# A transformer-like layer on one core: batch 1's T4 sums last and on GpSimd, other PSUM banks, an earlier slab split, moved down-stage casts

## The chip, the cores and the metric

The kernel runs on one core of one Trainium2 chip. The metric is the device time of one execution in microseconds. The engines are TensorE (PE in the profile; its weight loads are PEld), VectorE (DVE), ScalarE (ACT), GpSimd (POOL) and SyncE (SP), which issues nearly all DMAs. Each engine works through its own list of instructions in order, and waits on semaphores for the others.

## The reference

Two batches of 512 tokens, each of width 1024, go through one layer with shared weights; all is float32.

```python
xn = rmsnorm(x, norm1_g);  proj = xn @ w_in          # lru_x, lru_gate, q, k, v, gates
xc = dwconv(lru_x);  h = rglru_fwd(xc) + rglru_bwd(xc)
a_out = (gelu(lru_gate) * h) @ w_lru_out              # 1280 -> 1024
o = three dilated window attentions, combined by a softmax over their lse
b_out = o @ w_att_out                                 # 512 -> 1024
x = x + (sig(g_a) * a_out + sig(g_b) * b_out) @ w_o
xn2 = rmsnorm(x, norm2_g)
gate, val = split(xn2 @ w_up)                         # 1024 -> 3072 each
x = x + (gelu(dwconv(gate)) * val) @ w_down           # 3072 -> 1024
```

## The kernel before

Every product is made of three matmuls on pairs (hi, lo): each float32 operand is cast by ACT to a hi tile, and a subtraction on DVE or GpSimd makes the lo tile; then hi by hi, hi by lo and lo by hi are added up in PSUM (L1048 to L1050, L1196 to L1198, L1315 to L1317). Weights come as slabs of 128 by 512 through one stream, `ws`: `ws.adv(n)` splits up to n slabs ahead (load on SP, cast on ACT at L227, lo at L230 on the engine that `lo_eng` names in turn), at most eight slabs of a ring being alive and at most three loads ahead of the splits. `ws.take` hands them out and `ws.done` gives their place back.

The stages follow each other. The projections and the recurrence come first, then attention, then the gelu of the LRU gate with the combine of the three attention groups (`combine`, L872 to L879, the store of its result `o_d` at L879). These last steps are deferred functions, run by `tick()`; the loop `while later: tick()` drains them.

Then the mixing stage: `mix_tile(b, c)` makes, for each batch b and eight column tiles c, `a_out` and `b_out` in one two-bank PSUM tile (tag `m`, two buffers) and scales them with the gates `tha` and `thb` loaded by `th_load` (L980; DVE L1000 to L1004). `gain2`, the norm's gain for 128 partitions, is loaded at L1023. `o_phase` multiplies by `w_o` (`o_group`), and adds the result to the accumulator `acc[t]` of a tile of 128 tokens (DVE L1053). `load_acc` fills those accumulators with x.

The feed-forward part uses a scheme of seven products of half width for one 128-column tile f of gate and value (f from 0 to 23), in place of eight: for batch 0 the operands B11 and B21, for batch 1 sums of both batches called T1, T2, T3, T4 and B22. `batch0(f)` makes the products with B11 and B21, `rest(f, pa)` those with T2, T1, T3, B22 and T4, in this order, on PSUM banks of tag A, B and C. ACT copies between them: `u` (L1230) reads bank A after T2, and T3 writes that bank again; `p` (L1235) reads bank C after T1, and B22 writes it again. The weights of the products are sums too (L259, DVE), from four loads of `w_up` for each f (L245). From f = 0 to 3 (`EARLY`) batch 0's products come ahead of the others. After each product `prod` calls `ws.adv(2)`. The gelu (`gc`, L1243 to L1255) ends in the store of f's row to DRAM, `f_d` (L1256).

The operands of batch 1 are made tile by tile (four tiles of 128 tokens) in `sums_T`: eight transposes of the normalised tile into a two-bank PSUM tile `pst` (L1123), then sums by DVE and GpSimd (L1128) and casts by ACT (L1131 to L1148). It is a generator: each `sums(i)` runs tile i's next piece. `own_sums(i)` takes the squares for the norm (ACT L1014, whose output `junk` takes a PSUM tile of tag `m`), `own_scale(i)` applies it (DVE L1020). The table `after` and the lines ahead of the loop over f set which pieces stand between which products:

```python
6: lambda: (ws.adv(4), own_scale(2), sums(1, ps3, "m"), sums(0)),
7: lambda: (own_sums(3), sums(1), own_scale(3), lo_eng.remove(V), ws.adv(4)),
...
banks[0] = batch0(0, mid=lambda: (sums(2, ps4, "t"), sums(1)))
sums(2)
banks[1] = batch0(1)
sums(2)
sums(3, ps4, "t")
batch0(2, "C")
sums(3)
ws.hold = len(specs)
lo_eng[:] = [G]
batch0(3, "C", lambda: sums(3))
```

At the end, `h_fetch` loads rows of `f_d` again, `h_pair(f, engs)` casts two of them and makes their lo tiles (ACT L1272, L1273 on DVE for the first and GpSimd for the second), and the down stage multiplies them by `w_down` on eight PSUM banks (`psd`) and adds to the accumulators (DVE L1318).

Of the kernel before, what the change touches and what calls it, by code (L numbers as in the profile page):

```python
# [113 lines left out]
def layer_kernel(ctx: ExitStack, tc: tile.TileContext, xs_in, norm1_g, w_in, conv_w, conv_b, lru_wa, lru_ba,  # L114
# [791 lines left out]
    for c in range(KR):  # L906
# [43 lines left out]
        step[0] += 1  # L950
    while later:
        tick()
# [70 lines left out]
    SP.dma_start(out=gain2, in_=norm2_g[0].partition_broadcast(128))  # L1023
# [41 lines left out]
    lo_eng[:] = [V, G]  # L1065
    ws.adv(8)
    for c in range(KD):
        mix_tile(0, c)
        if c == 3:
            load_acc(0)  # L1070
    x2["B11"], x2["B21"] = half_pair(x20p, "B11"), half_pair(x20p, "B21")
# [46 lines left out]
    def sums_T(i, pst):  # L1118
# [7 lines left out]
        b12, b22, t1, t3 = v(pst[:, 0]), v(pst[:, 1]), v(x_t[:, 0:512]), v(x_t[:, 512:1024])  # L1126
        t2 = st.tile([128, 4, 128], F32, tag="t2", bufs=1, name="t2")
# [3 lines left out]
        A.copy(out=t3, in_=b12)  # L1131
        A.copy(out=hi("B22"), in_=b22)
        sub(V, t1, b12, hi("B11"))
        sub(V, t1, t1, lo("B11"))
        sub(V, t2, b22, t1)
        A.copy(out=hi("T1"), in_=t1)
        A.copy(out=hi("T2"), in_=t2)
        yield
        sub(V, t3, b22, t3)
        sub(V, lo("T1"), t1, hi("T1"))  # L1140
        sub(V, lo("T2"), t2, hi("T2"))
        sub(V, lo("B22"), b22, hi("B22"))
        A.copy(out=hi("T3"), in_=t3)
        sub(G, t1, hi("B21"), t2)
        sub(G, t1, t1, lo("B21"), ALU.add)
        sub(G, lo("T3"), t3, hi("T3"))
# [7 lines left out]
    def sums(i, pool=None, tag=None):  # L1154
# [13 lines left out]
        6: lambda: (ws.adv(4), own_scale(2), sums(1, ps3, "m"), sums(0)),  # L1168
# [13 lines left out]
    cm_ps, ps4 = open_pool("ps4", space=PSUM)  # L1182
    cm_ps_ab, ps4ab = open_pool("ps4ab", space=PSUM)
# [3 lines left out]
    g0s, p1 = {}, {}  # L1187

    def prod(ps, slab, op, start, free=True):
# [9 lines left out]
        if free:  # L1199
            ws.done("a", 1)  # L1200
            ws.adv(2)

    bank = lambda nm: (ps4 if nm == "C" else ps4ab).tile([128, 512], F32, tag=nm, bufs=2, name="pf" + nm)
# [15 lines left out]
    def rest(f, pa):  # L1219
# [16 lines left out]
        prod(pa, ws.take(1)[0], "T3", False)  # L1236
        V.tensor_tensor(out=p5, in0=p5, in1=pa, op=ALU.add)
# [40 lines left out]
    banks[0] = batch0(0, mid=lambda: (sums(2, ps4, "t"), sums(1)))  # L1278
    sums(2)
    banks[1] = batch0(1)  # L1280
    sums(2)
    sums(3, ps4, "t")
    batch0(2, "C")
    sums(3)
    ws.hold = len(specs)
    lo_eng[:] = [G]
    batch0(3, "C", lambda: sums(3))
    close(cm_st)
    for f in range(NF):
        if f == NF - 1:  # L1290
            for j in range(4):
                h_fetch(j)
        pa = banks.get(f) if f < EARLY else batch0(f)
        if f == NF - 1:
            h_pair(0, (V, G))
# [68 lines left out]
```

## Time and profile before

| | |
|---|---|
| time, median of three runs (lowest to highest) | 2123.88 us (2123.47 to 2126.91) |
| the profiled execution: time, and span in the trace | 2123.89 us, 2122.1 us |
| TensorE busy | 2032.0 us, 96% of the span |
| VectorE, ScalarE, GpSimd busy | 61%, 41%, 33% |
| HBM traffic over the span | 100 GB/s |
| chain that ended last, by engine | PE 75%, DVE 12%, issue 4%, ACT 4%, POOL 2%, DMA 2% |

All times in the rows are microseconds from the start of the span. An engine's busy share says how much of the span it worked; where TensorE is idle, the row that follows the gap names in brackets how long it sat idle and what released it.

### The profile page before, as it was taken

How to read it: one execution, taken by the hardware profiler on the slowest of the kernel's cores; microseconds unless marked ns; L12 is line 12 of the kernel's file. 1: busy time of each engine (PE TensorE's matmuls, PEld its weight loads, DVE VectorE, ACT ScalarE, POOL GpSimd, SP SyncE). 2: the span in 40 equal slices, each digit the busy share in tenths (PEclk: the TensorE clock that was granted, in tenths of full speed). 3: DMA queues.
4: the chain of work that ended last, by engine and by line, in shares of the span. 5: the costliest groups of instructions: out<-in, count | busy, mean ns of one | idle time of the engine just before them, and what ended most of it. 6: DMA issues, size and time to landing. Idle time of an engine off the chain costs nothing.

```text
span 2122.1 us, 26424 instructions
## 1 busy us (share of the span) xinstructions
PE 2032.0 (96%) x9571; PEld 1710.5 (81%) x9571; DVE 1296.6 (61%) x1874; ACT 873.1 (41%) x1501; POOL 691.7 (33%) x583
## 2 busy tenths in 40 slices
PE   8988898999999999999998999979999999999999
PEld 6866676787899999998776888757888888788887
DVE  5599998617862671575565565656555555465555
ACT  4488888622331243135442342433444444421210
POOL 3111111034113421423332122464545554532421
PEclk9999999999999999999999999989999999999999
DMA  4535444411111111103546556323222222352322
GB/s 146 156 99 143 115 127 131 158 45 43 34 41 46 40 51 55 35 16 120 163 159 209 170 165 196 106 76 92 89 75 85 90 80 90 121 196 80 109 90 80
DMA packets 204032, 218.71 MB, mean 103 GB/s; under 512 B 28892, under 2 KB 148222, under 8 KB 203902
## 3 DMA queue, kind: packets, MB, share of 16 engines
q1 hardware_dynamic: 201854, 211.78, 32.2%
q0 software_dynamic: 2048, 5.25, 1.0%
q8 instruction: 75, 1.23, 0.2%
q14 instruction: 55, 0.45, 0.1%
HBM read 161.73 MB, written 50.00 MB: 100 GB/s over the span
## 4 chain that ended last, share of the span: by engine, by line
PE 75%; DVE 12%; issue 4%; ACT 4%; POOL 2%; DMA 2%; SPq 0%; DVEq 0%; POOLq 0%; ACTq 0%
PE ps L807 7%; PE ps L808 6%; PE ps L809 6%; PE ps L151 5%; PE ps L152 5%; PE ps L153 5%; PE psd L1315 4%; PE psd L1317 4%; PE psd L1316 4%; PE pfA L1196 4%; PE pfA L1197 3%; PE pfA L1198 3%; DVE u L486 3%; PE o L728 3%; PE pfC L1196 2%
## 5 line engine op out<-in xcount | busy, mean ns | idle before, releaser
L230 POOL TENSOR_TENSOR lo<-raw,hi 128x512 fp32r<-128x512 f32 (+1 forms) x261 | 344.6, 1331 | 668.1 <-ACT hi L227 635.4
L227 ACT CAST hi<-raw 128x512 fp32r<-128x512 f32 (+1 forms) x352 | 204.8, 606 | 310.0 <-PE psd L1317 152.5
L807 PE MATMUL ps<-hi,xh 128*128 128x512 f32 x576 | 251.4, 437 | 0.0
L808 PE MATMUL ps<-lo,xh 128*128 128x512 f32 x576 | 228.5, 397 | 0.0
L809 PE MATMUL ps<-hi,xl 128*128 128x512 f32 x576 | 228.3, 396 | 0.0
L151 PE MATMUL ps<-xh,hi 128*128 128x512 f32 x544 | 217.8, 400 | 0.3 <-DVE xc L403 0.3
L152 PE MATMUL ps<-xl,hi 128*128 128x512 f32 x544 | 216.1, 397 | 0.0
L153 PE MATMUL ps<-xh,lo 128*128 128x512 f32 x544 | 215.4, 396 | 0.0
L1318 DVE TENSOR_TENSOR accd<-accd,psd 128x512 f32<-128x512 f32 x192 | 130.1, 686 | 110.8 <-PE psd L1317 104.4
L807 PEld LDWEIGHTS ps<-hi,xh 128*128 128x128 f32 x576 | 156.2, 271 | 9.6
L808 PEld LDWEIGHTS ps<-lo,xh 128*128 128x128 f32 x576 | 158.4, 275 | 6.0
L809 PEld LDWEIGHTS ps<-hi,xl 128*128 128x128 f32 x576 | 156.4, 271 | 8.0
L1315 PE MATMUL psd<-hi,hp 128*128 128x512 f32 x384 | 149.7, 390 | 0.4 <-DVE gc L1255 0.4
L1316 PE MATMUL psd<-lo,hp 128*128 128x512 f32 x384 | 149.4, 389 | 0.0
L1317 PE MATMUL psd<-hi,hp 128*128 128x512 f32 x384 | 149.4, 389 | 0.0
L707 ACT ACTIVATE p<-p,nm 128x128 f32<-128x128 f32 (+1 forms) x192 | 81.7, 427 | 146.4 <-DVE nm L705 146.3
L629 DVE TENSOR_REDUCE ss<-sq 128x8 f32<-128x512 f32 x48 | 32.9, 685 | 163.7 <-ACT sq L626 163.7
L1196 PE MATMUL pfA<-T,hi 128*128 128x512 f32 x288 | 116.0, 403 | 15.4 <-ACT u L1230 9.0
L151 PEld LDWEIGHTS ps<-xh,hi 128*128 128x128 f32 x544 | 104.9, 193 | 24.5 <-issue 1.2
L153 PEld LDWEIGHTS ps<-xh,lo 128*128 128x128 f32 x544 | 104.7, 192 | 22.7
L152 PEld LDWEIGHTS ps<-xl,hi 128*128 128x128 f32 x544 | 104.9, 193 | 22.1
L1198 PE MATMUL pfA<-T,lo 128*128 128x512 f32 x288 | 115.3, 400 | 0.9 <-POOL lo L230 0.9
(255 smaller groups left out, 4532.2 us busy)
## 6 DMA issues: line engine op xcount, KB each, us to landing
raw<-in_w_in_dram SPq DMA_DIRECT2D x144, 256.0 KB
raw<-in_w_up_dram SPq DMA_DIRECT2D x56, 256.0 KB
r<-in_w_up_dram SPq DMA_DIRECT2D x48, 256.0 KB
f_d<-gc SPq DMA_DIRECT2D x24, 512.0 KB
raw<-in_w_down_dram SPq DMA_DIRECT2D x48, 256.0 KB
hraw<-f_d SPq DMA_DIRECT2D x24, 512.0 KB
sg_d<-sgt SPq DMA_DIRECT2D x16, 512.0 KB
raw<-in_w_lru_out_dram SPq DMA_DIRECT2D x32, 256.0 KB
```

Of the source, the lines that this page charges most:

```text
L151: PE.matmul(out=ps, lhsT=a, rhs=b, start=(k == 0), stop=False)
L152: PE.matmul(out=ps, lhsT=a, rhs=rl(k), start=False, stop=False)
L153: PE.matmul(out=ps, lhsT=wl(k), rhs=b, start=False, stop=(k == n - 1))
L227: A.copy(out=hi[:, 0:n], in_=r[:, 0:n])
L230: e.tensor_tensor(out=lo[:, 0:n], in0=r[:, 0:n], in1=hi[:, 0:n], op=ALU.subtract)
L807: PE.matmul(out=ps, lhsT=a, rhs=hi, start=(k == 0), stop=False)
L808: PE.matmul(out=ps, lhsT=a, rhs=lo, start=False, stop=False)
L809: PE.matmul(out=ps, lhsT=b, rhs=hi, start=False, stop=(k == KD - 1))
L1196: PE.matmul(out=ps, lhsT=a, rhs=bh[:, k], start=(start and k == 0), stop=False, **kw)
L1315: PE.matmul(out=ps, lhsT=hh[:, i, tl], rhs=w[0], start=(i == 0), stop=False)
L1316: PE.matmul(out=ps, lhsT=hh[:, i, tl], rhs=w[1], start=False, stop=False)
L1317: PE.matmul(out=ps, lhsT=hl[:, i, tl], rhs=w[0], start=False, stop=(i == 1))
```

## The change

The change has four parts.

1. **Mixing start.** `lo_eng` is set to DVE and GpSimd in turn before the deferred functions are drained, and `ws.adv(8)` is called there too, besides the call at the old place. `gain2` is loaded not at L1023 but behind `load_acc(0)`, in the fourth tile of batch 0. In what is issued, one cast, one DVE lo and one LRU half-slab load (128 KB, ahead of the two `o_d` stores and one `y_d` store on SP) come earlier.
2. **Sums of batch 1.** The pieces of `sums_T` are cut anew. First DVE makes t1 and t2, ACT copies bank 0 to t3 and casts T1 and T2, and DVE makes T2's and T1's lo; second come B22 and T3, with both lo tiles on DVE; third two GpSimd sums for T4; last T4's cast and its lo on GpSimd. Before, the two T4 sums and T3's lo were one piece. t3 has a tile of its own and t2 takes half of the token tile. The calls of the pieces stand in other places, with the T4 pieces of tiles 1 to 3 ahead of `rest(0)`.
3. **Banks and pace.** In place of two PSUM pools there are four, opened in the order C, B, t, A. `prod` advances the stream by `pace[0]`: 1 in `batch0(0)` to `batch0(2)`, 2 in `batch0(3)`, 1 in `rest(0)` to `rest(3)`, and 2 from f = 4.
4. **Down-stage casts.** `h_pair(0, (V, G))` is called inside `rest(23)`, behind the T3 product, and no longer ahead of `rest(23)`.

The core of the diff:

```diff
+    lo_eng[:] = [V, G]
+    ws.adv(8)
     while later:
...
-    SP.dma_start(out=gain2, in_=norm2_g[0].partition_broadcast(128))
     def norm2_tile(t):
...
-    lo_eng[:] = [V, G]
             load_acc(0)
+            SP.dma_start(out=gain2, in_=norm2_g[0].partition_broadcast(128))
...
             PE.transpose(out=pst[:, k // 4, 128 * (k % 4):128 * (k % 4) + 128], in_=x_t[:, 128 * k:128 * k + 128],
                          identity=ident)
         v = lambda ap: ap.rearrange("p (k t) -> p k t", t=128)
-        b12, b22, t1, t3 = v(pst[:, 0]), v(pst[:, 1]), v(x_t[:, 0:512]), v(x_t[:, 512:1024])
-        t2 = st.tile([128, 4, 128], F32, tag="t2", bufs=1, name="t2")
+        b12, b22, t1, t2 = v(pst[:, 0]), v(pst[:, 1]), v(x_t[:, 0:512]), v(x_t[:, 512:1024])
+        t3 = st.tile([128, 4, 128], F32, tag="t3", bufs=1, name="t3")
         sub = lambda eng, out, x, y, op=ALU.subtract: eng.tensor_tensor(out=out, in0=x, in1=y, op=op)
         hi = lambda nm: x2[nm][0][:, :, tl]
         lo = lambda nm: x2[nm][1][:, :, tl]
-        A.copy(out=t3, in_=b12)
-        A.copy(out=hi("B22"), in_=b22)
         sub(V, t1, b12, hi("B11"))
         sub(V, t1, t1, lo("B11"))
         sub(V, t2, b22, t1)
+        A.copy(out=t3, in_=b12)
         A.copy(out=hi("T1"), in_=t1)
         A.copy(out=hi("T2"), in_=t2)
+        sub(V, lo("T2"), t2, hi("T2"))
+        sub(V, lo("T1"), t1, hi("T1"))
         yield
+        A.copy(out=hi("B22"), in_=b22)
         sub(V, t3, b22, t3)
-        sub(V, lo("T1"), t1, hi("T1"))
-        sub(V, lo("T2"), t2, hi("T2"))
+        A.copy(out=hi("T3"), in_=t3)
         sub(V, lo("B22"), b22, hi("B22"))
-        A.copy(out=hi("T3"), in_=t3)
+        sub(V, lo("T3"), t3, hi("T3"))
+        yield
         sub(G, t1, hi("B21"), t2)
         sub(G, t1, t1, lo("B21"), ALU.add)
-        sub(G, lo("T3"), t3, hi("T3"))
         yield
         A.copy(out=hi("T4"), in_=t1)
         sub(G, lo("T4"), t1, hi("T4"))
...
-        6: lambda: (ws.adv(4), own_scale(2), sums(1, ps3, "m"), sums(0)),
+        6: lambda: (ws.adv(4), own_scale(2), sums(1, ps3, "m")),
         7: lambda: (own_sums(3), sums(1), own_scale(3), lo_eng.remove(V), ws.adv(4)),
...
-    cm_ps, ps4 = open_pool("ps4", space=PSUM)
-    cm_ps_ab, ps4ab = open_pool("ps4ab", space=PSUM)
+    cm_pf, pf = zip(*(open_pool("ps4" + nm, space=PSUM) for nm in "CBtA"))
+    pf = dict(zip("CBtA", pf))
+    pace = [1]
     def prod(ps, slab, op, start, free=True):
...
-            ws.adv(2)
-
-    bank = lambda nm: (ps4 if nm == "C" else ps4ab).tile([128, 512], F32, tag=nm, bufs=2, name="pf" + nm)
+            ws.adv(pace[0])
+
+    bank = lambda nm: pf[nm].tile([128, 512], F32, tag=nm, bufs=2, name="pf" + nm)
     def batch0(f, nm="A", mid=None):
...
-    def rest(f, pa):
+    def rest(f, pa, mid=None):
...
         prod(pa, ws.take(1)[0], "T3", False)
+        if mid:
+            mid()
...
 
     ws.loads()
     banks = {}
-    banks[0] = batch0(0, mid=lambda: (sums(2, ps4, "t"), sums(1)))
+    banks[0] = batch0(0, mid=lambda: sums(2, pf["t"], "t"))
     sums(2)
     banks[1] = batch0(1)
+    sums(3, pf["t"], "t")
+    sums(0)
+    sums(0)
+    batch0(2, "C")
+    ws.hold = len(specs)
+    pace[0] = 2
+    lo_eng[:] = [G]
+    sums(1)
+    batch0(3, "C", lambda: sums(3))
+    sums(1)
     sums(2)
-    sums(3, ps4, "t")
-    batch0(2, "C")
+    sums(2)
     sums(3)
-    ws.hold = len(specs)
-    lo_eng[:] = [G]
-    batch0(3, "C", lambda: sums(3))
+    sums(3)
     close(cm_st)
+    pace[0] = 1
     for f in range(NF):
         if f == NF - 1:
             for j in range(4):
                 h_fetch(j)
+        if f == EARLY:
+            pace[0] = 2
         pa = banks.get(f) if f < EARLY else batch0(f)
-        if f == NF - 1:
-            h_pair(0, (V, G))
-        rest(f, pa)
-    close(cm_f, cm_b, cm_ps_ab, cm_ps)
+        rest(f, pa, (lambda: h_pair(0, (V, G))) if f == NF - 1 else None)
+    close(cm_f, cm_b, *cm_pf[::-1])
 
 
     cm_ps, ps5 = open_pool("ps5", space=PSUM)
```

How the instructions move, at three places.

ACT ahead of `rest(0)`, before. T4's casts are the rows with T4; `u2` is the copy of bank A between T2 and T3; `hi` rows are weight casts, those from `s1`, `s2` and `r21` of weight sums:

```order
L1211 COPY p1_11640<-pfC_11612 128x512
L1148 CAST T4_11028<-acc_10704 128x4x128
L227 CAST hi_11656<-r21_11464 128x512
L227 CAST hi_11668<-raw_11462 128x512
L227 CAST hi_11691<-r22_11466 128x512
L227 CAST hi_11699<-s2_11696 128x512
L1230 COPY u2_11676<-pfA_11468 128x512
L227 CAST hi_11718<-s1_11695 128x512
```

And after:

```order
L227 CAST hi_11664<-raw_11462 128x512
L1150 CAST T4_11028<-acc_10700 128x4x128
L1150 CAST T4_11028<-acc_10702 128x4x128
L1150 CAST T4_11028<-acc_10704 128x4x128
L227 CAST hi_11697<-r22_11466 128x512
L1233 COPY u2_11682<-pfA_11468 128x512
L227 CAST hi_11718<-s2_11715 128x512
```

Before, one T4 cast (tile 3's) stands there, five rows ahead of `u2`. After, three T4 casts (tiles 1 to 3) stand in a row, with one weight cast between them and `u2`. On GpSimd, T4's sums and lo of tiles 1 to 3 with four weight lo's among them are the operations behind tile 0's T4 lo.

SP around the store of f = 3's row, before. `f_d` rows are the stores of the rows 2, 3; the `w_up` rows between are loads for f = 5, those behind for f = 6:

```order
L245 DMA r22_11950<-in_w_up_dram 128x4x128
L1256 DMA f_d_68<-gc_12008 128x1024
L245 DMA raw_12076<-in_w_up_dram 128x4x128
L245 DMA raw_12095<-in_w_up_dram 128x4x128
L245 DMA r21_12097<-in_w_up_dram 128x4x128
L245 DMA r22_12099<-in_w_up_dram 128x4x128
L1256 DMA f_d_68<-gc_12119 128x1024
L245 DMA raw_12228<-in_w_up_dram 128x4x128
```

And after, with the loads of f = 5 behind both stores:

```order
L245 DMA r22_12016<-in_w_up_dram 128x4x128
L1261 DMA f_d_68<-gc_11988 128x1024
L1261 DMA f_d_68<-gc_12101 128x1024
L245 DMA raw_12147<-in_w_up_dram 128x4x128
L245 DMA raw_12153<-in_w_up_dram 128x4x128
L245 DMA r21_12155<-in_w_up_dram 128x4x128
L245 DMA r22_12157<-in_w_up_dram 128x4x128
L245 DMA raw_12234<-in_w_up_dram 128x4x128
L245 DMA raw_12253<-in_w_up_dram 128x4x128
```

Two stores stand side by side now; the four loads for f = 5 moved from between them to behind the second.

TensorE at the start of the down stage, with the semaphores waited on. Before, the fourth group of six matmuls begins with the wait for DVE, which is the gelu's last product:

```order
L1316 MATMUL psd<-lo,hp 128x512
L1317 MATMUL psd<-hi,hp 128x512
L1315 MATMUL psd<-hi,hp 128x512 [waits DVE_49]
L1316 MATMUL psd<-lo,hp 128x512
L1317 MATMUL psd<-hi,hp 128x512
```

And after, where it is the second group that begins with it:

```order
L1329 MATMUL psd<-lo,hp 128x512 [waits Pool_49]
L1330 MATMUL psd<-hi,hp 128x512 [waits Pool_49]
L1328 MATMUL psd<-hi,hp 128x512 [waits DVE_49]
L1329 MATMUL psd<-lo,hp 128x512
L1330 MATMUL psd<-hi,hp 128x512
```

The matmuls are the same ones; the wait moved from the nineteenth to the seventh.

## Rows read from the trace of the kernel before

**Rows 1.** The page, busy time, share of the span and instructions of TensorE

```profile
PE 2032.0 (96%) x9571; PEld 1710.5 (81%) x9571; DVE 1296.6 (61%) x1874; ACT 873.1 (41%) x1501; POOL 691.7 (33%) x583
```

**Rows 2.** Stretches: length, busy (count) PE, PEld, DVE, ACT, POOL; clock, DMA share, GB/s

```profile
1131.00:1133.00 2.00, 2.00 (x6) 1.61 (x5) 1.67 (x2) 1.60 (x4) 1.63 (x2) 0.50 0.32 98
...
1470.00:1842.00 372.00, 372.00 (x1643) 308.04 (x1642) 206.67 (x255) 157.06 (x253) 187.72 (x137) 1.00 0.28 84
...
1120.80:1123.80 3.00, 0.00 (x0) 0.00 (x0) 0.00 (x0) 0.00 (x0) 0.00 (x0) 0.98 0.68 217
...
1123.80:1126.80 3.00, 0.00 (x0) 0.00 (x0) 0.00 (x0) 0.40 (x1) 0.22 (x1) 0.50 1.03 317
```

**Rows 3.** Timeline at the mixing start: start, us, engine, line, operation, count, idle before it

```profile
1119.09 0.42 SPq L1023 DMA_DIRECT2D gain<-in_norm_g_dram  x1
...
1127.51 0.69 DVE L230 TENSOR_TENSOR lo<-raw,hi 128x512 fp32r<-128x512 f32 x1 [8.28 <-ACT hi L227]
...
1129.54 0.77 PE L151 MATMUL ps<-yh,hi 128*128 128x512 f32 x1 [8.97 <-DVE thb L1001]
```

**Rows 4.** Timeline, DVE, ACT and TensorE while tiles 0 to 2 are summed

```profile
1353.62 0.69 DVE L1128 TENSOR_TENSOR acc<-pst,B 128x512 f32<-128x512 f32 x1
...
1355.68 0.68 DVE L1053 TENSOR_TENSOR acc<-acc,pso 128x512 f32<-128x512 f32 x1
...
1356.47 1.03 ACT L1014 ACTIVATE junk<-acc 128x1024 f32<-128x1024 f32 x1
...
1357.77 1.03 PE L1123 MATMUL pst<-ident,acc 128*128 128x128 f32 x8
...
1364.51 0.68 DVE L1128 TENSOR_TENSOR acc<-pst,B 128x512 f32<-128x512 f32 x1
...
1366.97 0.68 DVE L1053 TENSOR_TENSOR acc<-acc,pso 128x512 f32<-128x512 f32 x1
...
1369.33 1.91 PE L1123 MATMUL pst<-ident,acc 128*128 128x128 f32 x8 [5.05 <-ACT junk L1014]
```

**Rows 5.** Timeline from tile 3's transposes to T3 of the first rest

```profile
1382.08 1.07 PE L1123 MATMUL pst<-ident,acc 128*128 128x128 f32 x8 [1.82 <-DVE B L1128]
...
1385.04 1.28 POOL L1128 TENSOR_TENSOR acc<-acc,B 128x512 f32<-128x512 f32 x1
...
1396.62 1.72 POOL L1128 TENSOR_TENSOR T<-acc,T 128x512 fp32r<-128x512 f32 x1
...
1397.13 1.76 DVE L259 TENSOR_TENSOR r<-raw,r 128x512 f32<-128x512 f32 x1
...
1397.91 0.79 PE L1196 MATMUL pfA<-T,hi 128*128 128x512 f32 x1 [3.83 <-ACT hi L227]
...
1410.53 0.80 PE L1196 MATMUL pfA<-T,hi 128*128 128x512 f32 x1 [3.56 <-ACT u L1230]
```

**Rows 6.** Timeline, TensorE's stalls in the second and third rest

```profile
1429.40 0.50 PE L1196 MATMUL pfA<-T,hi 128*128 128x512 f32 x1 [3.46 <-ACT u L1230]
...
1461.40 0.60 PE L1196 MATMUL pfA<-T,hi 128*128 128x512 f32 x1 [2.04 <-DVE u L1228]
```

**Rows 7.** Timeline, two loads of w_up and the first sum that uses them

```profile
1404.21 0.92 SPq L245 DMA_DIRECT2D r<-in_w_up_dram  x2
...
1407.92 0.69 DVE L259 TENSOR_TENSOR s<-r,r 128x512 f32<-128x512 f32 x1 [6.76 <-DMA r<-in_w_up_dram]
```

**Rows 8.** Timeline at the end of the feed-forward part and the down stage's start

```profile
1845.04 2.37 POOL L1273 TENSOR_TENSOR hp<-hraw,hp 128x1024 fp32r<-128x1024 f32 x1 [4.41 <-ACT hp L1272]
...
1845.39 0.58 ACT L1230 COPY u<-pfA 128x512 f32<-128x512 f32 x1
...
1846.02 0.50 PE L1196 MATMUL pfA<-T,hi 128*128 128x512 f32 x1 [1.96 <-ACT u L1230]
...
1847.14 0.62 ACT L227 CAST hi<-raw 128x512 fp32r<-128x512 f32 x1 [1.18 <-DMA raw<-in_w_down_dram]
...
1860.55 0.50 PE L1315 MATMUL psd<-hi,hp 128*128 128x512 f32 x1 [0.36 <-DVE gc L1255]
```

## The prediction

> **What bounds the kernel now.** I read the page first: TensorE is busy for 96% of the span [rows 1], so nothing off its path counts unless it makes TensorE wait. Then TensorE's work by stage [rows 2]: from 1470 to 1842 us it is busy in all of 372.00 us with 1643 matmuls, 0.2267 us each at full clock, and no edit can gain there. What is left are the places where TensorE stands still, which I took from the timeline with its releasers: the start of the mixing stage [rows 3], the start of the feed-forward part, where batch 1's operand sums are made [rows 4 to 6], and its end [rows 8]. Each stall has a second price: after it the granted clock is at the lower of its two levels (0.50 of 2.4 GHz from 1131 to 1133, with six matmuls started where 8.8 would have been) [rows 2]; eight transposes take 1.91 us behind the 5.05 us stall and 1.03 behind none [rows 4]. I count 1 to 2 us for each long stall, an estimate from these rows. TensorE's own order of work is the same after the change, so the sum is a sum of waits. It is made against the profiled execution's 2123.89 us (span 2122.1, 1.8 around it), which is the median of the runs shown to 0.01 us.
>
> **Mixing start: -3.0 us.** TensorE waits 8.97 us for two buffers that DVE frees, DVE for one cast's lo, the cast for the attention slab's load [rows 3]. Ahead of that load stand the 512 KB `gain2` and a 128 KB LRU half-slab. In the three microseconds in which mostly `gain2` moves, the queue carries 217 GB/s and TensorE is idle; behind it 317 [rows 2]. 512 KB are 1.7 us at the one rate and 2.4 at the other, the whole stretch is 3.0, and 128 KB are 0.4: the wait shortens by 2.0 to 3.4. What is issued earlier from the slab stream is little: one cast, one lo and that one 128 KB load. They stand before the combine's last operations, and delay them by at most their own 0.62 + 0.69. I take -3.0. `gain2` now goes behind the four accumulator loads of tile 3; TensorE has slabs split ahead there and the operand is wanted 75 us later, so I cost it at nothing; with the cover gone it would be the 3 us again. A wait of about 6 us stays, so the clock falls as before.
>
> **Sums for tiles 0 to 2: +6 us.** Before, DVE makes t1, t1, t2 and at once adds the output product to the accumulator (1353.62 to 1355.68, three operations in 2.06) [rows 4]. After, ACT's three casts (0.62 each) and two more DVE operations (0.69) stand between: 1.86 + 1.38 = 3.2 us later. The squares (1.03, ACT) need that sum, and tile 1's transposes need the bank that they free; before, they came 0.27 us behind the squares [rows 4]. So a new stall of 2.9 us. The tail of the piece also crosses to ACT and back: the B22 cast stands behind the squares, the t3 sum behind that cast, and T3's lo behind another cast, some 1.3 us more before DVE reaches the next tile. The same round trip (3.2) is in tile 1's piece, ahead of the sum at 1366.97 which tile 2's transposes wait for [rows 4]. Against this stands that they no longer wait for the squares: 2.36 us from that sum to the transposes become 0.75, so 1.6 comes back, and some 0.9 comes back because T4's sums no longer run on GpSimd beside DVE's double-length 1.04 to 2.31 us operations. Tile 2's transposes come 2.9 + 1.3 + 2.7 - 1.6 - 0.9 = 4.4 later. From there to tile 3's were 12.75 us (1369.33 to 1382.08) [rows 4, 5]; now DVE waits in turn for squares and cast (1.7), makes three (2.0), scales (1.3 to 2.3), makes three (2.1), waits for four casts (2.1), makes five (3.4 to 5.5 beside GpSimd): 12.6 to 15.7. I take 14.3, so +1.6. Together +6.0, between +3 and +8.5. The other banks for the transposes cost nothing by themselves; they only name a later reader.
>
> **From there to T3 of `rest(0)`: +1.0 us.** Before it took 28.45 us (1382.08 to 1410.53), with stalls of 3.83 and 3.56 in it [rows 5]. After, T2's weights are split in time, because the stream is advanced by one instead of two and four sums piece calls stand elsewhere. But on ACT the copy of `u` now stands behind the T4 casts of tiles 1, 2 and 3, each of which waits for GpSimd; T3 needs the bank that this copy frees. GpSimd has, from tile 0's T4 lo on, 13 operations before that last cast: that lo, two sums for each of three tiles, four weight lo's and two more T4 lo's. One takes 1.28 alone, 1.72 beside DVE [rows 5]. The first can begin when tile 3's three DVE sums (2.1) and four casts (2.5) are done, behind transposes of 1.07. That is 1.07 + 4.6 + 13 x 1.28 + two cast round trips (1.4) + the last cast and the copy (1.3) = 25.0 us, or 30.7 with all thirteen at 1.72. TensorE's own work from transposes to T3 is 1.07 + 72 matmuls x 0.2267 = 17.4 us, so the wait is 7.6 to 13.3 us, in place of 3.83, 3.56 and smaller ones. I take 29.5, in the upper part: the weight sums on DVE, the longest at 1.76, run in the same stretch [rows 5]. The bounds are -3.4 and +2.3. The Trainium skill (SBUF — State Buffer, Who interferes with whom) says that a DVE operation with two SBUF inputs and a GpSimd operation that reads SBUF exclude each other whole, and that issue order decides who blocks. The rows agree (1.72 and 1.76 side by side, against 1.28 and 0.69). By that rule eight weight sums of 0.69 would add 5.5 us to the 25.0, which gives 30.5, and the sum would be 1.0 higher.
>
> **`rest(1)` and `rest(2)`: -5.5 us.** Stalls of 3.46 and 2.04 us end on ACT's and DVE's `u` [rows 6], behind weight sums that came early. With the slower pace those stand further back. I leave 1 us of the 5.5 and give back 1 us of clock. Bounds -7.5 and -3.
>
> **Start of f = 4: +4.0 us.** What the smaller pace takes is lookahead: the four `w_up` loads of f = 5, which stood ahead of the store of f = 3's row, now stand behind it on SP, and that store waits for the gelu. At the end of the part the gelu's product is ready some 4.4 us behind T4's last matmul (18 matmuls of 0.2267 and the 0.36 stall) [rows 8]. Two loads take 3.7 us from first issue to use [rows 7]; the rate of 317 GB/s [rows 2] makes 0.83 of each 256 KB and 1.65 of the store. The fourth load is there 4.4 + 2.0 + 1.65 + 3.3 = 11.4 us after T4. Two DVE sums, the S2 cast and the `u` copy follow (0.69 + 0.69 + 0.62 + 0.58 = 2.6): 14.0 us. TensorE has four products of 12 matmuls until then, 10.9 us. A wait of 3.1, or 1.4 if store and loads overlap fully, and 1 us of clock. Bounds 0 and +6.
>
> **End of the part: +2.5 us.** The stall of 1.96 us behind `u` goes: ACT no longer holds the two `hp` casts in front of it [rows 8], and about 1 us of clock goes with it, -3.0. What comes: the copy of `p` now stands behind the cast of a slab that lands at about 1847.1 [rows 8], while TensorE would be at B22 1.96 us earlier than before, at 1846.6: the copy ends 1848.3, so +1.7. DVE's add for T4 stands behind the two `hp` casts and one lo, +1.0. GpSimd's `hp` lo of 2.37 [rows 8] now runs beside the gelu's DVE operations. Last, with the other bank order the down products meet the gelu's banks in their second group and not in their fourth: 12 matmuls of cover, 2.7 us, are gone. -3.0 + 1.7 + 1.0 + 2.7 = +2.4, with a little for GpSimd. Bounds -2 and +6.
>
> The sum is -3.0 + 6.0 + 1.0 - 5.5 + 4.0 + 2.5 = +5.0: 2128.9 us.
>
> **Rivals.** (1) Faster: GpSimd's chain before T3 of `rest(0)` runs at 1.28 an operation, because ACT and TensorE leave DVE little to do there, and DVE takes T3's lo without delaying the tiles. Then the two sums terms are +3 and -3.4, and with -5.5, -3, f = 4 at 0 and the end at +1 the sum is -7.9: 2116.0. For it speak 1.28 at 1385.04; against it 1.72 at 1396.62 [rows 5]. It decides where GpSimd needs under 1.4 us each. (2) No difference: the sums as I have them, but f = 4 has its loads in time and the end costs nothing: +6 + 1 - 5.5 - 3 = -1.5, 2122.4. For it speaks that each lookahead is several slabs; against it that the store stands ahead of the loads. (3) Worse: each exchange between ACT and DVE ends at its upper bound, +8.5 + 2.3 - 3 + 6 + 6 - 2 = +17.8: 2141.7. (4) The change doesn't do what it says at the mixing start: only one split is earlier, and if `gain2` were not what delays the slab, the 9 us stay: +3.0 on any of these, 2131.9 on the forecast.
>
> **How the numbers follow.** Two tenths of a per cent, 4.2 us, is about what a measurement here can tell from no change; that is 2119.6 to 2128.1. The forecast, with (4) in it, has 0.50 and its own range is 2124 to 2134; a fifth of it lies within 0.2%. Rival (1) has 0.25, (2) 0.17, (3) 0.08. So faster 0.25, same 0.10 + 0.17 = 0.27, slower 0.40 + 0.08 = 0.48. The range takes in the middle of (1) with 2 us of its own spread, and stops short of (3): 2114 to 2138.
>
> **What would show it.** In the profile of the changed kernel: a mixing stall of about 6 us; stalls before tiles 1, 2 and 3's transposes of about 3, 6 and 4 us, released by ACT's squares, a DVE accumulator sum and a DVE B22 lo; a single stall of 8 to 11 us before T3 of `rest(0)`, released by ACT's `u`, with T4 casts that wait for GpSimd right before it; one of some 3 us at f = 4 near 1475 to 1490; near 1855 to 1860 a wait of over 3 us for the gelu's product. Without the wait before T3 the forecast is wrong by up to 6 us, without those at f = 4 and at the end by up to 7.

## The result, and the profile after

The changed kernel is slower: its time is 1.0063 times that of before, with an interval of 1.0043 to 1.0084, which is 13 us (9 to 18) on 2123.7. One of its four runs, of 2429.65 us, was disturbed and is left out of the ratio; the others took 2135.22, 2137.24 and 2139.99 us. The profiled execution is the one of 2135.22 us, with a span of 2133.4 us, 11.3 us more than before.

TensorE has the same instructions as in [rows 1] and 1.3 us more busy time, so 10.0 of the 11.3 us are idle time. (A matmul at the lower clock counts as busy for longer; such stretches came and went at several places, and nearly cancel.) On the page, TensorE's busy time, share and instructions:

```profile
PE 2033.3 (95%) x9571; PEld 1710.6 (80%) x9571; DVE 1305.2 (61%) x1878; ACT 872.3 (41%) x1501; POOL 685.5 (32%) x579
```

In the timeline of the changed kernel (start, length, engine, line, operation, count, and in brackets the idle time before it with its releaser), TensorE's longer waits from the mixing start to the down stage are these:

```profile
1128.24 0.77 PE L151 MATMUL ps<-yh,hi 128*128 128x512 f32 x1 [9.12 <-DVE thb L1003]
...
1359.08 1.09 PE L1124 MATMUL pst<-ident,acc 128*128 128x128 f32 x8 [2.70 <-ACT junk L1016]
...
1372.48 0.90 PE L1124 MATMUL pst<-ident,acc 128*128 128x128 f32 x3 [5.22 <-DVE acc L1054]
...
1375.61 0.76 PE L1199 MATMUL pfB<-B,hi 128*128 128x512 f32 x1 [1.16 <-ACT T L1143]
...
1388.01 1.06 PE L1124 MATMUL pst<-ident,acc 128*128 128x128 f32 x8 [1.46 <-ACT T L1143]
...
1416.78 0.79 PE L1199 MATMUL pfA<-T,hi 128*128 128x512 f32 x1 [10.24 <-ACT u L1233]
...
1486.16 0.80 PE L1199 MATMUL pfA<-T,hi 128*128 128x512 f32 x1 [5.58 <-ACT u L1233]
...
1854.67 0.50 PE L1199 MATMUL pfC<-B,hi 128*128 128x512 f32 x1 [1.85 <-ACT p L1238]
...
1866.62 0.79 PE L1328 MATMUL psd<-hi,hp 128*128 128x512 f32 x1 [3.23 <-DVE gc L1260]
```

The row at 1128.24 answers to [rows 3]; 1359.08, 1372.48 and 1388.01 are the transposes of [rows 4, 5], where tile 1's had no wait and now have 2.70 us; 1416.78 is T3 of `rest(0)`, with 10.24 us in place of 3.56; the stalls of 3.83 [rows 5] and of 3.46 and 2.04 us [rows 6] are gone; 1486.16, T3 of f = 4, had no wait before; nor had 1854.67, B22 of f = 23, nor 1866.62, where the second group of down products waits for the gelu that the fourth waited for before [rows 8]. One thing in front of this has to be put right: a rest is 60 matmuls, and the stall of 2.04 us at 1461.40 stands 180 behind T3 of `rest(0)`. So it is T3 of `rest(3)`, the fourth rest, and not of the third.

Since TensorE's order is the same, each of its matmuls can be set against the same one before. How much later it starts, in the two profiled executions:

| matmul | before | after | later by |
|---|---|---|---|
| first of the mixing stage behind its wait | 1129.54 | 1128.24 | -1.30 |
| tile 1's transposes | 1357.77 | 1359.08 | +1.31 |
| tile 2's | 1369.33 | 1372.48 | +3.15 |
| tile 3's | 1382.08 | 1388.01 | +5.93 |
| T3 of `rest(0)` | 1410.53 | 1416.78 | +6.25 |
| T3 of `rest(3)` | 1461.40 | 1461.30 | -0.10 |
| nine matmuls on, at full clock again | 1465.12 | 1463.42 | -1.70 |
| T3 of f = 4 | 1482.14 | 1486.16 | +4.02 |
| ten matmuls on, at full clock again | 1484.41 | 1490.42 | +6.01 |
| B22 of f = 23 | 1850.25 | 1854.67 | +4.42 |
| second group of down products | 1857.30 | 1866.62 | +9.32 |
| last matmul | 2117.74 | 2129.01 | +11.28 |

The loss is made in three places: +7.2 from the mixing stage's start to tile 3's transposes, +7.7 around f = 4, +5.3 at the end. Between them 8.0 us come back in `rest(0)` to `rest(3)`.

**Between tile 2's transposes and tile 3's**, three of DVE's rows in the changed kernel, and a stretch with TensorE's clock:

```profile
1376.16 2.32 DVE L1022 SCALAR_TENSOR_TENSOR acc<-acc,sr,gain 128x1024 f32<-128x1024 f32 x1
...
1382.66 3.41 DVE L1129 TENSOR_TENSOR T<-acc,T 128x512 fp32r<-128x512 f32 x2 [1.77 <-ACT T L1137]
1385.99 0.67 DVE L1219 TENSOR_TENSOR g<-p,pfB 128x512 f32<-128x512 f32 x1
...
1371.00:1380.90 9.90, 7.26 (x21) 5.72 (x22) 7.99 (x10) 4.80 (x9) 5.53 (x5) 0.50 0.36 110
```

The scale and the two lo's (1.71 and 1.77 us) run beside GpSimd rows, and TensorE counts 21 matmuls where 38 were.

**Ahead of T3 of `rest(0)`**, ACT's and GpSimd's rows:

```profile
1393.62 1.29 POOL L1129 TENSOR_TENSOR T<-acc,T 128x512 fp32r<-128x512 f32 x1 [8.11 <-ACT T L1150]
...
1403.34 0.62 ACT L1150 CAST T<-acc 128x512 fp32r<-128x512 f32 x1
...
1409.38 0.62 ACT L1150 CAST T<-acc 128x512 fp32r<-128x512 f32 x1 [5.42 <-POOL acc L1129]
...
1411.70 1.71 POOL L1129 TENSOR_TENSOR acc<-B,acc 128x512 f32<-128x512 f32 x1
1413.48 1.59 POOL L1129 TENSOR_TENSOR acc<-acc,B 128x512 f32<-128x512 f32 x1
...
1415.10 0.62 ACT L1150 CAST T<-acc 128x512 fp32r<-128x512 f32 x1 [5.11 <-POOL acc L1129]
...
1416.15 0.58 ACT L1233 COPY u<-pfA 128x512 f32<-128x512 f32 x1
```

Two T4 casts stand idle for 5.42 and 5.11 us behind GpSimd's sums, and the copy of `u` is queued behind them. GpSimd's chain begins at 1393.62 with tile 0's T4 lo and has 13 operations up to the sum of 1413.48. They take 18.9 us together: seven take 1.26 to 1.30 us each and six, which run beside DVE rows, 1.59 to 1.75.

**Around f = 4**, DVE, SP and ACT:

```profile
1460.58 15.00 SPq L1261 DMA_DIRECT2D f_d<-gc  x2
...
1474.27 0.88 DVE L1258 TENSOR_TENSOR gc<-gc,p 128x512 f32<-128x512 f32 x1
...
1475.62 2.36 SPq L245 DMA_DIRECT2D raw<-in_w_up_dram  x2
...
1482.63 1.54 DVE L259 TENSOR_TENSOR s<-r,r 128x512 f32<-128x512 f32 x1 [6.69 <-DMA r<-in_w_up_dram]
...
1485.53 0.58 ACT L1233 COPY u<-pfA 128x512 f32<-128x512 f32 x1
```

SP's row of 1460.58 holds two stores: the first at once, the second only when gc's last product (DVE, 1474.27 plus 0.88) is there. All loads for f = 5 come after it, the first weight sum 7.0 us after the first load, and `u` behind the cast of the slab that this sum is needed for.

**The clock.** Stretches behind the waits of 5.58 and 3.23 us (length; busy time and count of PE, PEld, DVE, ACT, POOL; clock; DMA share; GB/s), in the changed kernel:

```profile
1487.00:1491.00 4.00, 4.00 (x12) 3.10 (x12) 0.00 (x0) 0.79 (x3) 2.72 (x3) 0.60 0.04 9
1868.00:1872.00 4.00, 4.00 (x11) 3.06 (x10) 0.00 (x0) 0.00 (x0) 2.09 (x1) 0.50 1.02 300
```

And the first of them before:

```profile
1487.00:1491.00 4.00, 4.00 (x20) 3.30 (x19) 2.68 (x4) 2.05 (x3) 1.29 (x1) 1.00 0.06 18
```

TensorE is busy all the time in each, but counts 12 and 11 matmuls where 20 and 19 were (19 from 1868 to 1872 before): the granted clock is 0.60 and 0.50 of full speed, that is, at the lower of its two levels (1.2 of 2.4 GHz) for most of the one stretch and all of the other. It costs some 2 us behind each wait: T3 of f = 4 starts 4.02 us later than before and the matmul ten places on 6.01.

**The mixing start.** DVE, ACT and SP in the changed kernel, then stretches of it, then two of the kernel before, which lie the same 0.42 us ahead of its last combine store:

```profile
1108.39 1.77 DVE L230 TENSOR_TENSOR lo<-raw,hi 128x512 fp32r<-128x512 f32 x1
...
1111.42 1.28 ACT L865 ACT_TABLE_LOAD   x1 [5.55 <-DVE cd L864]
...
1119.42 0.32 SPq L879 DMA_DIRECT2D o_d<-cg  x1
...
1120.80 0.38 SPq L216 DMA_DIRECT2D raw<-in_w_att_out_dram  x1
...
1125.56 0.62 ACT L227 CAST hi<-raw 128x512 fp32r<-128x512 f32 x1 [11.28 <-DMA raw<-in_w_att_out_dram]
```

```profile
1119.00:1122.00 3.00, 0.12 (x1) 0.00 (x0) 0.00 (x0) 0.00 (x0) 2.29 (x3) 0.93 0.53 156
1122.00:1125.00 3.00, 0.00 (x0) 0.00 (x0) 0.00 (x0) 0.00 (x0) 0.00 (x0) 0.50 0.97 258
1125.00:1128.00 3.00, 0.00 (x0) 0.00 (x0) 1.79 (x3) 0.62 (x1) 0.00 (x0) 0.50 0.96 325
```

```profile
1118.29:1121.29 3.00, 2.28 (x11) 1.55 (x9) 0.94 (x1) 0.00 (x0) 2.09 (x2) 1.00 0.50 173
1121.29:1124.29 3.00, 0.00 (x0) 0.00 (x0) 0.00 (x0) 0.00 (x0) 0.00 (x0) 0.90 0.67 222
```

The combine's last store is issued 0.71 us later than before (1118.71). The earlier split does this by its lo on DVE (1108.39, 1.77 us), which stands ahead of the combine's first operation there, and not by its cast: ACT has stood idle for 5.55 us, waiting for DVE, when the combine's exponent begins with its table load (1111.42). The slab's cast starts 6.1 us after that store, 2.0 less than before. The queue carries 156, 258 and 325 GB/s in the three stretches, and 173 and 222 in the first two before: its first microseconds are slow with or without `gain2`.

TensorE's wait is no shorter: 9.12 us, where 8.97 were and about 6 forecast. It ends 1.30 us earlier, but TensorE also comes to it 1.45 us earlier, since the kernel before ran at a granted clock of 0.50 from 1073 to 1075 and the changed one at 1.00. So this pair of executions alone doesn't give the size. The fourteen traces of this case do: from the issue of the combine's last loads to the first mixing matmul it takes 29.7 to 30.3 us in the eight kernels without the first part and 28.2 to 28.7 in the six with it, 1.5 us less.

### The profile page after: what moved, and what is told of

Its sections match the earlier page's. It is cut to its first block, busy times and chain, and to the rows that moved or that the text cites. A ratio compares the mean times of both kernels' runs of the same rounds, so it can differ in the third digit from the quotient of the medians.

```text
span 2133.4 us, 26417 instructions
## 1 busy us (share of the span) xinstructions
PE 2033.3 (95%) x9571; PEld 1710.6 (80%) x9571; DVE 1305.2 (61%) x1878; ACT 872.3 (41%) x1501; POOL 685.5 (32%) x579
## 4 chain that ended last, share of the span: by engine, by line
PE 75%; DVE 12%; ACT 5%; issue 4%; POOL 2%; DMA 1%; SPq 0%; DVEq 0%; POOLq 0%; ACTq 0%
PE ps L807 7%; PE ps L808 6%; PE ps L809 6%; PE ps L151 5%; PE ps L153 5%; PE ps L152 5%; PE psd L1328 4%; PE psd L1330 4%; PE psd L1329 4%; PE pfA L1199 3%; PE pfA L1200 3%; PE pfA L1201 3%; DVE u L486 3%; PE o L728 3%; PE pfC L1199 2%
```

## The experiments

First the parts alone, each put into the kernel before; the third part is taken as two, pools and pace.

**The mixing start alone** (e1_mix): the first three hunks of the diff.

> The kernel before with the first part alone (earlier split, gain2 behind the accumulator loads). Theory: the combine's last store comes some 0.7 us later, because one cast stands ahead of its exponent, and the attention slab lands some 2 us earlier against that store; the first mixing matmul comes 1.3 us earlier, and the time falls by 1 to 2 us (2122 to 2123). Rival, the prediction's own term: 3.0 us less (2120.9). Nothing changes behind the mixing stage: the stalls before the transposes stay at about 5.0 and 1.8 us.

Measured: 2122.11 us against 2123.20, ratio 0.9997 (0.9986 to 1.0008). In the trace the first mixing matmul starts at 1128.63, 0.9 earlier, and 8.7 us after the combine's last store in place of 10.8. The time can't be told from no change: the interval holds the theory's 1 to 2 us and reaches to the rival's 3.0 at its end. It is the trace that speaks for the theory. The earlier split and the move of `gain2` were not run apart.

**The moved casts alone** (e2_hpair):

```diff
...
-        if f == NF - 1:
-            h_pair(0, (V, G))
-        rest(f, pa)
+        rest(f, pa, (lambda: h_pair(0, (V, G))) if f == NF - 1 else None)
```

> The kernel before with the fourth part alone (the first two hp casts behind T3 of the last rest). Theory: the 1.96 us wait for u goes; waits of 1.5 to 2 us before B22 (behind the copy of p) and 1 to 2 before T4 come in its place; the down products have 18 matmuls of cover for the gelu, so that their wait is 1 to 2 us and not 3.4. Net 0 to +3 us (2124 to 2127). Rival: the casts' place alone makes the whole loss at the end, +5 us (2129), whatever the bank order.

Measured: 2123.31 us, ratio 1.0000 (0.9991 to 1.0009). TensorE's waits at the end, in the timeline of this kernel:

```profile
1849.12 0.50 PE L1196 MATMUL pfC<-B,hi 128*128 128x512 f32 x1 [1.31 <-ACT p L1235]
...
1852.93 0.50 PE L1196 MATMUL pfA<-T,hi 128*128 128x512 f32 x1 [0.79 <-DVE p L1239]
...
1860.75 0.50 PE L1315 MATMUL psd<-hi,hp 128*128 128x512 f32 x1 [0.71 <-DVE gc L1257]
```

The 1.96 us wait for `u` is exchanged for 1.31 + 0.79 and the wait behind the gelu grows from 0.36 to 0.71. Each wait is a little shorter than expected. Nothing is won, nothing lost: the theory holds, the casts' place alone does not make the loss at the end.

**The pools alone** (e4_banks): in place of `ps4` and `ps4ab` the four pools, opened in the order C, B, t, A.

> The kernel before with the four PSUM pools in the order C, B, t, A alone. Theory: the down products meet the gelu's banks in their second group, the wait there grows from 0.36 to about 3 us (12 matmuls of cover less) and the clock drops behind it for another 1 to 2.5 us: 2126 to 2129. The transposes of tiles 2 and 3 wait for other readers: within 1 us. Rival: the loss in the changed kernel needs the moved casts too; then the wait is under 1.5 us and the time 2123 to 2125.

Measured: 2126.34 us, ratio 1.0019 (1.0009 to 1.0029). Tile 2's transposes and the second group of down products:

```profile
1367.61 0.69 PE L1123 MATMUL pst<-ident,acc 128*128 128x128 f32 x2 [3.41 <-DVE acc L1053]
...
1858.16 0.80 PE L1315 MATMUL psd<-hi,hp 128*128 128x512 f32 x1 [3.07 <-DVE gc L1255]
```

The wait behind the gelu is 3.07 us and not 0.36, with the casts where they were: the theory holds. In the trace this end costs 3.9 us, counted against the kernel before from T4 of f = 23 to the last matmul. At the transposes the new banks give 1.6 us (3.41 in place of 5.05, and the releaser is DVE's sum, not ACT's squares), and all of it goes again in a new wait of 1.60 before B21.

**The smaller pace alone** (e3_pace): `ws.adv(pace[0])` in `prod`, with 1, 2, 1 and 2 at the places of the change.

> The kernel before with the smaller pace alone (1 in the first three batch-0 products and in rest(0) to rest(3)). Theory: the four loads for f = 5 move behind the store of f = 3's row, and TensorE waits 4 to 6 us before T3 of f = 4 with 1 to 2 us of clock behind it; the stalls of 3.5 and 2.0 us in rest(1) and rest(2) go; net -1 to +4 us (2123 to 2128). Rival: the wait at f = 4 comes from the late T4 casts and sums, not from the pace; then there is none here, and the time falls by 4 to 8 us (2116 to 2120).

Measured: 2119.78 us, ratio 0.9981 (0.9972 to 0.9991): faster. TensorE's wait at f = 4, and SP's stores ahead of it:

```profile
1449.23 14.98 SPq L1257 DMA_DIRECT2D f_d<-gc  x2
...
1475.11 0.80 PE L1197 MATMUL pfA<-T,hi 128*128 128x512 f32 x1 [5.82 <-ACT u L1231]
```

Both halves of the theory are in the trace: by f = 3 TensorE is 13 us ahead of the kernel before, since the stalls of 3.56, 3.46 and 2.04 us and their clock are gone; then the second store holds SP up, T3 of f = 4 waits 5.82 us, and with the clock 8 us are given back. The pace alone is enough for the wait at f = 4, so the rival is out. The net, though, is on the good side of what I expected.

**The sums alone** (e5_sums): the changed kernel with the pools, the pace, the mixing start and the casts of before; only the pieces of `sums_T` and their places are new.

> The changed kernel with the other three parts undone: the new pieces of the sums and their places alone, on the old banks and with the pace of 2. Theory: stalls of 3, 5.5, 1.5 and 1.6 us in the tiles' sums, one of 8 to 11 us before T3 of rest(0) behind the T4 casts, and no wait at f = 4; the time is 2126 to 2133. Rival: with the pace of 2 the T4 casts on ACT and the weights' casts exchange places, so that the stall before T3 is under 5 us, and the time is 2119 to 2125.

Measured: 2134.96 us, ratio 1.0054 (1.0039 to 1.0069). Three of its waits:

```profile
1376.06 0.69 PE L1123 MATMUL pst<-ident,acc 128*128 128x128 f32 x2 [6.48 <-ACT junk L1014]
...
1390.36 0.45 PE L1123 MATMUL pst<-ident,acc 128*128 128x128 f32 x1 [3.21 <-ACT T L1142]
...
1420.57 0.80 PE L1199 MATMUL pfA<-T,hi 128*128 128x512 f32 x1 [10.84 <-ACT u L1233]
```

The theory's side, and above its upper end of 2133. This part alone loses nearly all that the change loses; with the old bank tile 2's transposes wait for the squares as well, 6.48 us. The five alone make -1.1 + 0.1 + 3.9 - 3.4 + 11.8 = +11.3 us, against 13 for all together. Each is known to some 2 or 3 us and the whole to 4.5, so the sum agrees with the whole, but no more can be said.

Then single causes, taken out of the changed kernel.

**T4's sums on DVE** (a_t4dve):

```diff
-        sub(G, t1, hi("B21"), t2)
-        sub(G, t1, t1, lo("B21"), ALU.add)
+        sub(V, t1, hi("B21"), t2)
+        sub(V, t1, t1, lo("B21"), ALU.add)
```

> The changed kernel with the two T4 sums of each tile on DVE and not on GpSimd (T4's lo stays on GpSimd). Theory: GpSimd's chain ahead of the copy of u loses six operations of 1.3 to 1.7 us; the wait of 10.4 us before T3 of rest(0) falls to 2 to 6 us, the time by 4 to 8 us (2130 to 2134). Rival: the casts on ACT wait for the w_up loads and not for GpSimd; then the wait stays at 8 us or more and the time within 2 us.

Measured: 2129.24 us, ratio to before 1.0025 (1.0015 to 1.0034), so some 8 us less than the changed kernel, and just under the theory's range. The last T4 cast and T3:

```profile
1408.18 0.62 ACT L1150 CAST T<-acc 128x512 fp32r<-128x512 f32 x1 [2.75 <-DVE acc L1129]
...
1409.86 0.65 PE L1199 MATMUL pfA<-T,hi 128*128 128x512 f32 x1 [3.45 <-ACT u L1233]
```

The wait falls from 10.24 to 3.45 us, and the cast waits 2.75 us, for DVE now. GpSimd's chain made the greater part of the wait, and the rival is out. Some 2 of the 8 us come from earlier: the wait ahead of tile 3's transposes (1.46 us) is gone too.

**The old pools in the changed kernel** (a_banks).

> The changed kernel with the two PSUM pools of before. Theory: the fourth group of down products and not the second meets the gelu's banks, 12 matmuls or 2.7 us later; the wait of 3.23 us there falls to 0.5 to 1.5 us and the clock does not drop behind it; 3 to 5 us less than the changed kernel (2133 to 2135). Rival: the casts and lo's of the down stage set the wait, whatever the banks; then 3 us stay and the time is that of the changed kernel (2138).

Measured: 2131.12 us, ratio 1.0031 (1.0020 to 1.0042), some 6 to 7 us less, which is more than expected.

```profile
1868.42 0.50 PE L1329 MATMUL psd<-hi,hp 128*128 128x512 f32 x1 [0.73 <-DVE gc L1261]
```

The wait of 3.23 us falls to 0.73 and the clock stays up behind it (1.00 from 1869 to 1873). From T4 of f = 23 to the last matmul this kernel loses 0.3 us against the kernel before, where the changed one loses 5.4.

**The pace back earlier** (b_pace_f3 and b_pace_f2): e3_pace with `if f == EARLY - 1:` and `if f == EARLY - 2:` ahead of `pace[0] = 2`.

> The kernel before with the smaller pace alone, as in e3_pace, but back to 2 at f = 3 and not at f = 4. Theory: loads for f = 5 go ahead of the store of f = 3's row again, and the 6 us wait before T3 of f = 4 with its 2 us of clock is gone or below 1.5 us: 2112 to 2115. Rival: one f is too short to rebuild the lookahead, the wait only moves or halves: 2116 to 2119.

> The same with the pace back to 2 at f = 2. Theory: no wait at f = 4, but the weight sums of rest(2) and rest(3) come early again and part of the 2 us stall before u returns: 2112 to 2117. Rival: the lookahead is limited by eight slabs in any case and nothing differs from b_pace_f3 by over 1 us.

Measured: 2118.96 (0.9976, 0.9965 to 0.9986) and 2117.33 us (0.9968, 0.9957 to 0.9979), which can't be told from e3_pace. The longest wait behind `rest(0)` in the one and in the other:

```profile
1457.79 0.76 PE L1197 MATMUL pfC<-B,hi 128*128 128x512 f32 x1 [3.75 <-ACT hi L227]
```

```profile
1442.59 0.47 PE L1197 MATMUL pfA<-T,hi 128*128 128x512 f32 x1 [2.69 <-DVE u L1229]
```

At f = 4 there is no wait now, but one stands before B22 of f = 3, or before T3 of f = 2. I had expected it to go; the rival of b_pace_f3 is right, it moves. The stall before `u` returned is the one that b_pace_f2's theory named. So the loads' place behind the store can't be the whole cause.

**The store moved behind the loads** (c2_store): on e3_pace, the store of f = 3's row is kept back and issued after `batch0(4)`.

```diff
-        SP.dma_start(out=f_d[128 * f:128 * f + 128, :], in_=gc.rearrange("p b t -> p (b t)"))
+        st_row = lambda f=f, gc=gc: SP.dma_start(out=f_d[128 * f:128 * f + 128, :], in_=gc.rearrange("p b t -> p (b t)"))
+        held_row.append(st_row) if f == EARLY - 1 else st_row()
...
         pa = banks.get(f) if f < EARLY else batch0(f)
+        while held_row:
+            held_row.pop()()
...
```

> e3_pace with one line more: the store of f = 3's row is issued behind batch 0's two products of f = 4, so that the four w_up loads of f = 5 go ahead of it on SP again. Theory: the 6 us wait before T3 of f = 4 comes from these loads standing behind the store; it falls to 0 to 2 us, its 2 us of clock go too, and the time is 2112 to 2115 (5 to 8 us less than e3_pace). Rival: the wait is a debt of weight sums and casts that the smaller pace put off, as the two kernels with an earlier return to 2 suggest, where it only moved; then 4 to 6 us stay somewhere between f = 3 and f = 5, and the time is 2117 to 2120.

Measured: 2116.12 us, ratio 0.9972 (0.9963 to 0.9980). What SP waited for from 1449 to 1467 (in total, times, longest), then its last loads for f = 5 and T3 of f = 4:

```profile
SPq L245 <- POOL lo L230: 14.2, 2, 14.0
```

```profile
1464.73 1.25 SPq L245 DMA_DIRECT2D r<-in_w_up_dram  x2
...
1472.22 0.50 PE L1197 MATMUL pfA<-T,hi 128*128 128x512 f32 x1 [3.21 <-ACT u L1231]
```

About half of it is the store: the wait falls from 5.82 to 3.21 us, and the slow clock behind it costs 1.8 us in place of 2.1. The times alone don't show it, since the interval and that of e3_pace overlap. The other half is the loads' next obstacle: for 14.0 us SP waits until GpSimd has read the one buffer of `r21`, whose lo comes late. That the smaller pace put it late, and that a second buffer would end the wait, is read from the trace and was not run. Neither of the two expectations holds alone; the time lies between them.

**Mixing start and store together** (c3_mix_store): the first part put into c2_store.

> c2_store with the changed kernel's mixing start. Theory: the two add, 1 us less than c2_store: 2111 to 2114, which is below both kernels. Rival: the wait at f = 4 stays, 2116 to 2119.

Measured: 2114.69 us, ratio 0.9963 (0.9950 to 0.9976), the lowest median here and faster than both kernels; from c2_store the intervals don't part it. The wait at f = 4 is 3.22 us, as in c2_store.

**Three causes out at once** (a_all3): old pools, T4's sums on DVE and the kept-back store in the changed kernel.

> The changed kernel with three things of it taken back at once: the old PSUM pools, T4's two sums on DVE, and the store of f = 3's row behind batch 0's two products of f = 4. Theory: the three removals add. One by one they gave 7.5 us (old banks), 9.4 us (T4 on DVE) and, on another base, 3.7 us (store): 20 us less than the changed kernel, 2116 to 2121, with the waits before the transposes of tiles 1 to 3 left (3, 6 and 3 us). Rival: they overlap, what one gives back the next waits for, as the pace did when it came back earlier; then 2124 to 2131.

Measured: 2121.32 us, ratio 0.9990 (0.9980 to 1.0000): some 16 us less than the changed kernel, between the two expectations and nearer to the first. So with these three out, the changed kernel's net loss is gone.

```profile
1371.84 0.69 PE L1124 MATMUL pst<-ident,acc 128*128 128x128 f32 x2 [7.28 <-ACT junk L1016]
...
1409.07 0.50 PE L1200 MATMUL pfA<-T,hi 128*128 128x512 f32 x1 [3.44 <-ACT u L1234]
```

What one gives, another takes in part: with the old pools tile 2's transposes wait 7.28 us in place of 5.22, for the squares. The wait before T3 stays at 3.44, and that at f = 4 at 3.29.

## Why the prediction was right, and where its sizes were off

The direction was right, which had a chance of 0.48, and so were the places. The size was not: +13 us where +5.0 was forecast. The median of the three runs, 2137.24, is inside the range of 2114 to 2138 by less than 1 us, outside the forecast's own 2124 to 2134, and nearer to rival (3), 2141.7, than to 2128.9. That it is in the range is in part luck: four terms were 9.4 us too low together, two were 3.2 us too high, and the range was wide because it took in the middle of rival (1). Of the waits that were named, six have the releaser that was named: ACT's squares, DVE's accumulator sum, ACT's `u` behind T4 casts, `u` again at f = 4, ACT's `p`, the gelu's product. Two signs failed: the mixing stall is not 6 us, and tile 3's transposes wait 1.46 us and not 4, for ACT's T3 cast and not for DVE's B22 lo, which ended 0.06 us earlier. By the steps:

- **Mixing start, -3.0**: measured -1.3 in the profiled pair, and -1.5 over all traces. Two sizes were off. `gain2` was counted with the time in which it had the queue; 2.0 came back, as the lower bound had it, since the queue is as slow in its first microseconds without it. And the delay by the earlier split was bounded and then left out of the sum: its lo on DVE put the combine's last store off by 0.7. That one more split is issued early was right.
- **Sums for tiles 0 to 2, +6.0**: +7.2. Tile 1's stall is 2.70, and tile 2's transposes come 4.45 us later than the mixing start would have them, as worked out. (The sum has 2.7 for the second round trip where its text has 3.2; the rows give 2.65: from the tile's first DVE sum to the accumulator sum, 1364.51 to 1366.97 before and 1366.64 to 1371.75 after.) The 1.2 us that are missing lie between tile 2's transposes and tile 3's: 15.5 us where 14.3 was taken out of 12.6 to 15.7. In that chain DVE's scale took 2.32 us and T2's and T1's lo 1.71 and 1.77, and a sum of batch 0 (0.67) stood between them. TensorE needed most of that time itself, because it ran at the lower clock (0.50 from 1371 to 1380.9) and waited 1.16 us before B21; this is why the stall at tile 3 is small.
- **To T3 of `rest(0)`, +1.0**: +0.3. From tile 3's transposes to T3 it took 28.77 us where 29.5 was forecast. The chain by GpSimd is shown by the run that took the sums off it. It began at 1393.62, as worked out, and its 13 operations took 1.46 us each in the mean, between the 1.28 and the 1.72 of the bounds. With that, the working gives 27.3; GpSimd's waits of 1.28 and 0.53 us for casts of weight sums, which the working didn't have, make up the rest. The Trainium skill (SBUF — State Buffer, Who interferes with whom) says that DVE and GpSimd share one pair of ports as an exclusive lock, and that a DVE instruction with two SBUF inputs contends with a GpSimd instruction that reads SBUF. The rows of the run with the sums on DVE agree: a T4 sum on DVE took 0.69 us alone (1391.80), and the last three 1.63 to 1.78 beside GpSimd's lo's of 1.72 to 1.74. The Trainium skill (GPSIMD Engine Reference, Engine selection) also advises DVE for elementwise work on two inputs, GpSimd being about twice as slow. Here it is 0.69 to 1.27, and it mattered because the chain set an end.
- **`rest(1)` and `rest(2)`, -5.5**: -8.0, over `rest(0)` to `rest(3)`: the 2.04 us that the term ascribes to `rest(2)` stood in `rest(3)`, where the pace is 1 too. Both stalls are gone whole, and with them some 1.6 us of slow clock behind each, of which the sum had only 1 us altogether. The pace alone shows that the pace does it; with the new sums and the pace of 2 both stalls stay (4.28 and 2.71 us in e5_sums).
- **f = 4, +4.0**: +7.7. The working had 14.0 us from T4's end to the end of the copy; it was 16.6 (T4's end is 48 matmuls of 0.2267 before 1480.42, where T1's last ends; the copy ends at 1486.1), by gc's further operation for an early f and a first weight sum that took 1.54 in place of 0.69. The wait was 5.58 and not 3.1, and behind it the clock cost 2 and not 1. That the loads stand behind the store was about half of the cause; the other half, the single buffer of `r21`, was not in the working, and the pace's own gain hides it: alone, the pace is 3.4 us faster.
- **End, +2.5**: +5.3. The wait for `p` is 1.85, that for the gelu 3.23, as worked out. The +1.0 for DVE's add shows no wait of its own in the changed kernel. The step that failed is the clock, which I let go up by 1 us with the removed stall and counted nowhere behind the two new ones. From B22 to the second group TensorE loses 1.5 us to it, behind that group 2.0.

The end was too small by the clock alone, f = 4 by the wait's length (2.5) and by the clock (1): a stall of 2 to 6 us was priced at its length plus 1, and in these places it costs its length plus about 2. Rival (1), the faster one, failed because the exchanges between ACT and DVE did delay the tiles and the waits at f = 4 and at the end came; at its own point it was close, since seven of GpSimd's 13 operations needed under 1.4 us, but the mean was 1.46. Rival (2) failed at f = 4 and at the end, where both waits came. Rival (3) came nearer than the forecast, with f = 4 above its upper bound of 6 and the end near the same one, and its 0.08 was too little.

What stays open: why the slow clock behind waits of equal length lasts longer in one place than in another; what a second buffer of `r21` would bring; and what the changed pieces would bring with the squares moved ahead of them. Neither of the last two was tried.

## What to carry to other kernels

A chain that is off the critical path may become it when its pieces are gathered behind one another on a slow engine and a queue that others share stands behind it: ask of each operation put last who is queued behind its waits. Putting work off with a smaller lookahead gains at once and is paid for in part when the lookahead is used up, at the next store or buffer that loads stand behind; read SP's order there. Pools opened in another order choose which of the next stage's first tiles waits for the last stage's slowest reader.

## What the runs showed of the hardware that I had not expected

Behind a wait of 3.23 us TensorE ran at a granted clock of 0.50 from 1868 to 1872, with 11 matmuls in place of 19; behind one of 0.73 us (the old pools) it lost nothing. So the 2.7 us of cover that the old bank order gives were worth 5.0 us from T4 of f = 23 on in the changed kernel, and 3.9 us in the kernel before. The DMA queue, which had moved 3 GB/s from 1116 to 1119, moved 156 and 258 GB/s in the next two stretches of 3 us and 325 in the third, with several loads waiting.
